# The head of a two-layer encoder kernel: three small loads on another queue, the first weights in halves, first products and scaling on ScalarE, wide matmuls ahead of the narrow sums

## The chip, the cores and the metric

The kernel runs on one NeuronCore of a Trainium2 chip. The metric is the device time of one execution in microseconds (us), as the median of several runs. TensorE (PE) multiplies matrices, VectorE (DVE), ScalarE (ACT) and GpSimd (POOL) work on elements, and SyncE (SP) issues transfers from device memory. Each engine takes its instructions in the order of the program; semaphores order the engines among each other.

## The reference

Input x is 256 tokens by 1024 features, fp32; c is one conditioning vector of 1024. Two layers, each a SwiGLU FFN with half weight, a token mixer and a second FFN. Every sub-layer is wrapped as follows; `mod` comes from c.

```python
mod = (silu(c) @ ada_w[i] + ada_b[i]).reshape(B, 9, D)      # per layer: 9 vectors of 1024
def modulated_sublayer(x, mod, g_pre, g_post, fn, weight):  # shift, scale, gate = mod[0:3] of the sub-layer
    h = rmsnorm(x, g_pre) * (1.0 + scale) + shift
    y = rmsnorm(fn(h), g_post)
    return x + weight * (1.0 + gate) * y
def swiglu(h, w_in, w_out):
    gate, up = split(h @ w_in, 2)
    return (silu(gate) * up) @ w_out                        # w_in 1024 x 5632, w_out 2816 x 1024
```

The change touches only the head of the program: the first sub-layer's shift (vector 0) and scale (vector 1), the first h, and the first products of FFN 0.

## The kernel before

The 256 tokens are two blocks of 128 (t = 0, 1). The FFN's hidden units go in 11 chunks of 256 (c = 0 to 10); a chunk's `wi` weights come in two parts of 1 MB (q = 0: k of 0 to 3, q = 1: k of 4 to 7). Most matmuls are done in three fp32r products: a weight is cast to a high part on ScalarE (L263) and the rest is its low part, subtracted on VectorE (L271); h is split in the same way (L588, L590 and L593). The three products are L98 to L100. The first parts of chunks 0 and 2 (`task_in_whole`) are used unsplit as fp32 (L794).

A modulation vector is a product of silu(c) with a 1024 x 1024 block of `ada_w`. It is not done on TensorE. The rows of the block lie as (partition, k), and VectorE adds eight products of a weight tile with one column of `sc` (`ada_step`: k = 0 writes the accumulator at L350, k = 1 to 7 add to it at L352). Narrow matmuls of one column (`finish_cols`, L361) then sum over the partitions, and two small VectorE instructions (L374, L377) add bias and norm weight. In the head the vectors are made in halves of 512 columns (`ada_half`; hf = 0, 1), each in two loads of 1 MB (q = 0, 1): vectors 0 and 1, first halves, then their second halves.

h itself: ScalarE squares x and sums (L508), VectorE and GpSimd make the root (L501, L503), x is scaled to xr in halves on ScalarE (L554) and VectorE (L555), TensorE transposes it (`turn_half`, L562), and shift and scale are applied while it is read from PSUM, on ScalarE (L576) or VectorE (L582) (`mod_half`). The rest is cast and subtracted as above.

The order is written out by hand. `Bulk` holds a list of tasks (key, load, high, low). Loads are issued by SP in the order of the list, as soon as one of 4 buffers (`N_RAW`) is free; `until(key)` runs tasks up to one, and for each emits its high part (ScalarE) and its low part (VectorE). `finish_pe` emits the narrow sums of finished vectors, `finish` also the additions behind them. `head_first` emits the first four k of chunks 0, 1 and 2 for both blocks (12 of 24 products each in chunk 1; L794 for the others), and at each `next(halves)` goes on in the generator `first_halves`, which places the other work of the head between those products. `warm` emits products of the identity with itself that nobody reads (L108).

Of the kernel before, what the change touches and what calls it, by code (L numbers as in the profile page):

```python
# [11 lines left out]
F32 = mybir.dt.float32  # L12
# [5 lines left out]
P = 128  # L18
D = 1024
S = 256  # L20
NT = S // P
KD = D // P
# [17 lines left out]
def kernel(  # L40
# [71 lines left out]


    c_col = cpool.tile([P, KD], F32, name="c_col")
    nc.sync.dma_start(c_col, c_in.rearrange("o (p k) -> p (o k)", k=KD))
    xt = [rowp.tile([P, D], F32, tag=f"x{t}", name=f"x{t}", bufs=1) for t in range(NT)]

    def load_x(t):
        nc.sync.dma_start(xt[t], x_in[0, t * P : (t + 1) * P, :])
# [8 lines left out]
    mhalf = cpool.tile([P, 1], F32, name="mhalf")  # L128
    nc.vector.memset(mhalf, -0.5)
    sc = cpool.tile([P, KD], F32, name="sc")  # L130
    nc.scalar.activation(sc, c_col, AF.Silu)


    cols = cpool.tile([P, 96 + 144 + 3], F32, name="cols")
# [1 line left out]
    C_Q = 96 + 144  # L136
    C_KV = C_Q + 2

    def load_columns(parts, base):
        rows = rowp.tile([P, 512], F32, tag="bc", name="rows", bufs=4)[:, :P]  # L140
        n = 0
        for ap in parts:
            r = ap.shape[0]
            nc.sync.dma_start(rows[n : n + r, :], ap)
            n += r

        def turn():
            ps = tr_tile("ps_cols")
            nc.tensor.transpose(ps[:, :n], rows[:n, :], ident[:n, :n])
            nc.vector.tensor_copy(cols[:, base : base + n], ps[:, :n])  # L150

        return turn

    turn_g = load_columns([norm_g.rearrange("l m (j p) -> (l m j) p", p=P)], 0)
    turn_b = load_columns([ada_b[0:1, :].rearrange("l (r p) -> (l r) p", p=P)], C_B)

    def load_columns_late():
        return load_columns(
# [157 lines left out]
    def ada_half(layer, m, hf, accs, pieces=(1, 1)):  # L316
# [16 lines left out]
        def compute(q):  # L333
            def go():
                rv = st.pop(q).rearrange("p (k n) -> p k n", k=4)
                if m not in accs:
                    accs[m] = rowp.tile([P, D], F32, tag="acc", name=f"aacc{layer}{m}", bufs=3)
                acc = accs[m][:, hf * 512 : (hf + 1) * 512]
                for j in range(4):
                    ada_step(acc, rv[:, j, :], 4 * q + j)  # L340
                if q == 1:
                    bulk.fin.append(lambda: finish_cols(layer, m, range(hf * 4, hf * 4 + 4))(acc))

            return go

        return [(("adah", m, hf, q), load(q), None, compute(q)) for q in range(2)]

    def ada_step(acc, w, k):
        if k == 0:
# [265 lines left out]
    class FFN:  # L615
# [168 lines left out]
        def head_first(self, hT, h0, halves):  # L784
# [3 lines left out]
            for c in range(3):  # L788
                if c > 0:
                    a = acc_tile(c - 1, f"first{c}")  # L790
                for t in range(NT):
                    pss[c, t] = psum.tile([P, 512], F32, tag="in", name=f"in0{t}") if c == 0 else a[t]
                    for k in range(4) if c != 1 else ():
                        nc.tensor.matmul(  # L794
                            pss[c, t], lhsT=h0[t][:, k * P : (k + 1) * P], rhs=self.wi[c, 0][:, k, :],
                            start=k == 0, stop=False,
                        )
                    if c == 1:
                        self.mm_in(pss[c, t], c, t, hT[t], range(4))
                    next(halves)  # L800
# [528 lines left out]


    accs = {}
    first = ada_half(0, 0, 0, accs) + ada_half(0, 1, 0, accs, (1, 2))
    with_load = lambda t, f: (t[0], lambda: (t[1](), f()), *t[2:])
    first[1] = with_load(first[1], lambda: load_x(0))
    first[2] = with_load(first[2], lambda: load_x(1))
    h01, h11 = ada_half(0, 0, 1, accs), ada_half(0, 1, 1, accs, (1, 2))
    first += [f0.task_in_whole(0, 0), h01[0], f0.task_in(1, 0), h01[1], *h11, f0.task_in_whole(2, 0)]
    ss1 = shift_scale(0, 1)
    first += [f0.task_in(0, 1), ss1[0], f0.task_in(1, 1), ss1[1], f0.task_in(2, 1), f0.task_out(0)]
    first += [ss1[2], f0.task_out(1), ss1[3], f0.task_in(3, 0), f0.task_in(3, 1)]  # L1340
# [50 lines left out]
        )  # L1391


    bulk.until(("adah", 0, 0, 1))
    turn_g()
    turn_b()
    bulk.finish_pe()
    s20 = first_rstd(0)
    xr0 = pre_xr(0, s20)
    bulk.until(("adah", 1, 0, 0))  # L1400
    bulk.finish()
    s21 = first_rstd(1)
    xr1 = pre_xr(1, s21)
    hT = [new_hT(0), new_hT(1)]
    turned = [turn_half(0, 0, xr0)]
    warm(6, "acc11", 1)
    turned += [turn_half(1, 0, xr1, psum.tile([P, 512], F32, tag="acc10", name="ps_h10", bufs=1))]
    warm(4, "acc11", 1)
    bulk.until(("adah", 1, 0, 1))
    bulk.finish()  # L1410
    parts = [mod_half(t, 0, ps, hT[t], 0, 0, t == 1) for t, ps in enumerate(turned)]

    def first_halves():
        bulk.until(("adah", 0, 1, 0))
        yield
        for high, low, _ in parts:
            high()
            low()
        bulk.until(("wi", 0, 0, 1, 0))
        yield  # L1420
        bulk.until(("adah", 0, 1, 1))
        bulk.finish()
        late = [turn_half(0, 1, xr0)]
        yield
        yield
        bulk.until(("adah", 1, 1, 1))
        f0.high_in(0, 1)
        bulk.finish()
        late += [turn_half(1, 1, xr1)]
        late = [mod_half(t, 1, ps, hT[t], 0, 0, t == 0) for t, ps in enumerate(late)]  # L1430
# [2 lines left out]
        for _, low, _ in late:  # L1433
            low()
        yield
        yield

    f0.head_first(hT, [p[2] for p in parts], first_halves())
    turn_late = load_columns_late()
    f0.unit(3, 0, hT[0])  # L1440
    f0.unit(3, 1, hT[1])
# [238 lines left out]
```

## Time and profile before

| | us |
|---|---|
| median of 3 runs | 925.85 (924.13 to 928.99) |
| profiled execution | 930.35 |
| its span on the core | 928.6 |
| first wide matmul of FFN 0 starts | 24.04 |
| second halves' last narrow sums start | 44.09 |
| low part of wi01 starts on VectorE | 48.94 |

Times in the trace count from the start of the span. The profiled execution is one execution, 4.5 us above the median of the runs.

### The profile page before, as it was taken

What the parts mean: (1) busy time and instruction counts of PE and PEld (TensorE: products, weight loads), DVE (VectorE), ACT (ScalarE), POOL (GpSimd) and SP (SyncE); (2) the same over time, 40 slices, a digit from 0 to 9 for tenths busy, and PEclk for the clock granted to TensorE, in tenths of its full rate; (3) what the DMA queues carried; (4) which work ended last, traced back from release to release, by engine and by line L of the source; (5) the groups of instructions that cost most, each with busy time, mean ns of one, the idle gap of its engine ahead of it and who ended that gap; (6) DMA issues with size and microseconds to landing.
All of it is one profiled execution on the core that took longest, in us unless ns stands there. A gap on an engine that the chain in (4) does not pass through costs nothing.

```text
span 928.6 us, 11171 instructions
## 1 busy us (share of the span) xinstructions
PE 898.9 (97%) x4251; PEld 733.0 (79%) x4251; DVE 703.9 (76%) x848; ACT 437.3 (47%) x653; POOL 41.8 (5%) x56
## 2 busy tenths in 40 slices
PE   3999999999999999999999999999999999999997
PEld 3568887887888888888888888888776888888885
DVE  5798888887877898797867987766798765656553
ACT  2255443345645434334742534337698654343421
POOL 0000000000000000000000000001163000000000
PEclk9899999999999999999999999998999999999999
DMA  9989998996357999898469999961143458857601
GB/s 325 368 299 343 360 373 313 351 359 242 137 180 264 378 339 326 297 387 275 137 183 360 324 351 327 344 229 59 46 137 113 160 153 280 293 193 259 227 1 45
DMA packets 135973, 235.28 MB, mean 253 GB/s; under 512 B 5628, under 2 KB 98415, under 8 KB 135664
## 3 DMA queue, kind: packets, MB, share of 16 engines
q1 hardware_dynamic: 135920, 234.58, 72.8%
q8 instruction: 33, 0.54, 0.2%
q14 instruction: 20, 0.16, 0.1%
HBM read 233.51 MB, written 1.05 MB: 253 GB/s over the span
## 4 chain that ended last, share of the span: by engine, by line
PE 88%; DVE 7%; issue 2%; DMA 1%; ACT 1%; POOL 0%; SPq 0%; DVEq 0%; POOLq 0%; ACTq 0%
PE acc L747 25%; PE in L100 16%; PE in L98 16%; PE in L99 16%; PE accm L1319 2%; PE ps_g L724 2%; DVE aacc L352 1%; PE ps_h L562 1%; PE ps_mod L361 1%; PE in L794 1%; DVE nm L1220 1%; DVE ql L1203 1%; DMA wo<-in_ffn_w_out_dram 1%; PE accp L965 1%; DMA adah<-in_ada_w_dram 1%
## 5 line engine op out<-in xcount | busy, mean ns | idle before, releaser
L352 DVE SCALAR_TENSOR_TENSOR aacc<-ada,sc,aacc 128x1024 f32<-128x1024 f32 (+1 forms) x113 | 143.8, 1272 | 9.9 <-DMA ada<-in_ada_w_dram 7.6
L708 ACT ACTIVATE sil<-in 128x256 f32<-128x256 f32 x84 | 32.2, 383 | 247.0 <-PE in L100 242.1
L710 DVE TENSOR_TENSOR g<-in,sil 128x256 f32<-128x256 f32 x84 | 35.2, 419 | 52.0 <-ACT sil L708 51.9
L95 DVE TENSOR_TENSOR gL<-ps_g,gH 128x256 fp32r<-128x256 f32 x88 | 36.6, 416 | 23.6 <-ACT gH L94 23.5
L94 ACT CAST gH<-ps_g 128x256 fp32r<-128x256 f32 x88 | 32.4, 368 | 44.5 <-PE ps_g L724 44.4
L503 POOL TENSOR_TENSOR r<-ms,mhalf 128x1 f32<-128x1 f32 x24 | 13.6, 565 | 840.5 <-DVE ms L501 840.5
L724 PEld LDWEIGHTS ps_g<-ident,g 128*128 128x128 f32 x176 | 24.7, 140 | 11.5
L724 PE MATMUL ps_g<-ident,g 128*128 128x128 f32 x176 | 33.6, 272 | 0.0
L508 ACT ACTIVATE junk<-x 128x512 bf16<-128x512 f32 x24 | 15.1, 631 | 21.1 <-DVE x L535 11.3
L361 PE MATMUL ps_mod<-ones,aacc 128*128 128x1 f32 x96 | 12.9, 262 | 10.9 <-DVE cols L150 9.7
L361 PEld LDWEIGHTS ps_mod<-ones,aacc 128*128 128x128 f32 x96 | 13.2, 213 | 11.9 <-DVE cols L150 10.0
L576 ACT ACTIVATE hs<-ps_h,mod,mod 128x128 f32<-128x128 f32 x48 | 18.0, 456 | 8.6 <-DVE mod L377 5.5
L352 DVE SCALAR_TENSOR_TENSOR aacc<-adah,sc,aacc 128x512 f32<-128x512 f32 x28 | 21.0, 751 | 0.9
L582 DVE TENSOR_SCALAR hs<-ps_h,mod,mod 128x128 f32<-128x128 f32 x48 | 16.4, 403 | 4.9 <-PE ps_h L562 4.6
L535 DVE SCALAR_TENSOR_TENSOR x<-tmp,r,x 128x512 f32<-128x512 f32 x23 | 16.3, 748 | 2.2 <-POOL r L503 1.2
L1238 POOL TENSOR_SCALAR p<-p,rs 128x256 f32<-128x256 f32 x16 | 16.1, 1008 | 26.8 <-ACT p L1228 16.4
L1228 ACT ACTIVATE p<-s,nm 128x256 f32<-128x256 f32 x32 | 15.0, 478 | 4.0 <-DVE nm L1220 2.6
L554 ACT ACTIVATE xr<-x,r 128x512 f32<-128x512 f32 x12 | 8.7, 722 | 17.4 <-POOL r L503 17.4
L593 DVE TENSOR_TENSOR hTL<-hs,hTH 128x512 fp32r<-128x512 f32 x24 | 15.6, 689 | 0.4
L271 DVE TENSOR_TENSOR wo10L<-wo,wo10H 128x2048 fp32r<-128x2048 f32 x4 | 9.2, 2292 | 8.1 <-ACT wo10H L263 8.1
L397 DVE TENSOR_REDUCE mod<-ps_turn 128x4 f32<-128x512 f32 x12 | 8.2, 687 | 8.1 <-PE ps_turn L391 8.1
L562 PE MATMUL ps_h<-ident,xr 128*128 128x128 f32 x96 | 13.7, 283 | 0.5 <-ACT xr L554 0.3
(498 smaller groups left out, 2880.3 us busy)
## 6 DMA issues: line engine op xcount, KB each, us to landing
wi<-in_ffn_w_in_dram SPq DMA_DIRECT2D x176, 512.0 KB, 5.8
ada<-in_ada_w_dram SPq DMA_DIRECT2D x64, 1024.0 KB, 7.1
wo<-in_ffn_w_out_dram SPq DMA_DIRECT2D x44, 1024.0 KB, 6.4
adah<-in_ada_w_dram SPq DMA_DIRECT2D x6, 1024.0 KB, 10.3
mwo<-in_mla_w_o_dram SPq DMA_DIRECT2D x4, 1024.0 KB, 6.1
bc<-in_ada_b_dram SPq DMA_DIRECT2D x12, 256.0 KB, 6.8
bc<-in_norm_g_dram SPq DMA_DIRECT2D x12, 256.0 KB, 7.4
adah<-in_ada_w_dram SPq DMA_DIRECT2D x4, 512.0 KB, 11.7
```

The lines of the kernel that those rows point to most:

```text
L94: nc.scalar.copy(h, src)
L95: nc.vector.tensor_sub(lo, src, h.bitcast(F32))
L98: nc.tensor.matmul(ps, lhsT=lh, rhs=rh, start=first, stop=False)
L99: nc.tensor.matmul(ps, lhsT=lh, rhs=rl, start=False, stop=False)
L100: nc.tensor.matmul(ps, lhsT=ll, rhs=rh, start=False, stop=last)
L352: nc.vector.scalar_tensor_tensor(acc, w, sc[:, k : k + 1], acc, op0=ALU.mult, op1=ALU.add)
L361: nc.tensor.matmul(ps[:, j : j + 1], lhsT=acc[:, (j - j0) * P : (j - j0 + 1) * P], rhs=ones[:, 0:1], start=True, stop=True,)
L562: nc.tensor.transpose(ps[:, j * P : (j + 1) * P], xr[:, kk * P : (kk + 1) * P], ident)
L708: nc.scalar.activation(sil, ps[:, 0:CW], AF.Silu)
L710: nc.vector.tensor_mul(g, ps[:, CW : 2 * CW], sil)
L724: nc.tensor.transpose(ps[:, a * P : (a + 1) * P], g[:, a * P : (a + 1) * P], ident)
L747: nc.tensor.matmul(acc[hf], lhsT=lhs[:, a, :], rhs=rhs[:, a, hf * 512 : (hf + 1) * 512], start=f, stop=l)
```

## The change

The loads of c, of the norm weights and of the first layer's biases go from SP's queue to ScalarE's; the Silu is emitted after them. The transposes of norm weights and biases (`turn_g`, `turn_b`) come before the first modulation products. The first four modulation loads are each made in two pieces of 512 KB (the fourth already was), and x of block 1 is loaded after all of them. The product with k = 0 of the half vectors is made on ScalarE, as the task's high part. Both halves of xr are scaled on ScalarE. The ten identity products are replaced by five of 512 columns with x, all behind the transposes of block 0; the second block's root, scaling, transposes and shift come later, its transposes inside chunk 0 of `head_first`. In the list, `wi` chunk 1 comes ahead of vector 0's second half. In `first_halves` the narrow sums of the second halves and what hangs on them come one or two steps later: those of vector 0 after the first block of chunk 2, those of vector 1 after its second block.

```diff
--- before.py
+++ after.py
@@ -112,7 +112,7 @@
 
 
     c_col = cpool.tile([P, KD], F32, name="c_col")
-    nc.sync.dma_start(c_col, c_in.rearrange("o (p k) -> p (o k)", k=KD))
+    nc.scalar.dma_start(c_col, c_in.rearrange("o (p k) -> p (o k)", k=KD))
     xt = [rowp.tile([P, D], F32, tag=f"x{t}", name=f"x{t}", bufs=1) for t in range(NT)]
 
     def load_x(t):
@@ -128,7 +128,6 @@
     mhalf = cpool.tile([P, 1], F32, name="mhalf")
     nc.vector.memset(mhalf, -0.5)
     sc = cpool.tile([P, KD], F32, name="sc")
-    nc.scalar.activation(sc, c_col, AF.Silu)
 
 
     cols = cpool.tile([P, 96 + 144 + 3], F32, name="cols")
@@ -136,12 +135,12 @@
     C_Q = 96 + 144
     C_KV = C_Q + 2
 
-    def load_columns(parts, base):
+    def load_columns(parts, base, queue=nc.sync):
         rows = rowp.tile([P, 512], F32, tag="bc", name="rows", bufs=4)[:, :P]
         n = 0
         for ap in parts:
             r = ap.shape[0]
-            nc.sync.dma_start(rows[n : n + r, :], ap)
+            queue.dma_start(rows[n : n + r, :], ap)
             n += r
 
         def turn():
@@ -151,8 +150,10 @@
 
         return turn
 
-    turn_g = load_columns([norm_g.rearrange("l m (j p) -> (l m j) p", p=P)], 0)
-    turn_b = load_columns([ada_b[0:1, :].rearrange("l (r p) -> (l r) p", p=P)], C_B)
+    turn_g = load_columns([norm_g.rearrange("l m (j p) -> (l m j) p", p=P)], 0, nc.scalar)
+    turn_b = load_columns([ada_b[0:1, :].rearrange("l (r p) -> (l r) p", p=P)], C_B, nc.scalar)
+
+    nc.scalar.activation(sc, c_col, AF.Silu)
 
     def load_columns_late():
         return load_columns(
@@ -333,17 +334,20 @@
         def compute(q):
             def go():
                 rv = st.pop(q).rearrange("p (k n) -> p k n", k=4)
-                if m not in accs:
-                    accs[m] = rowp.tile([P, D], F32, tag="acc", name=f"aacc{layer}{m}", bufs=3)
                 acc = accs[m][:, hf * 512 : (hf + 1) * 512]
-                for j in range(4):
+                for j in range(q == 0, 4):
                     ada_step(acc, rv[:, j, :], 4 * q + j)
                 if q == 1:
                     bulk.fin.append(lambda: finish_cols(layer, m, range(hf * 4, hf * 4 + 4))(acc))
 
             return go
 
-        return [(("adah", m, hf, q), load(q), None, compute(q)) for q in range(2)]
+        def first():
+            if m not in accs:
+                accs[m] = rowp.tile([P, D], F32, tag="acc", name=f"aacc{layer}{m}", bufs=3)
+            nc.scalar.activation(accs[m][:, hf * 512 : (hf + 1) * 512], st[0][:, 0:512], AF.Copy, scale=sc[:, 0:1])
+
+        return [(("adah", m, hf, q), load(q), first if q == 0 else None, compute(q)) for q in range(2)]
 
     def ada_step(acc, w, k):
         if k == 0:
@@ -791,6 +795,8 @@
                 for t in range(NT):
                     pss[c, t] = psum.tile([P, 512], F32, tag="in", name=f"in0{t}") if c == 0 else a[t]
                     for k in range(4) if c != 1 else ():
+                        if c == 0 and t == 0 and k == 2:
+                            next(halves)
                         nc.tensor.matmul(
                             pss[c, t], lhsT=h0[t][:, k * P : (k + 1) * P], rhs=self.wi[c, 0][:, k, :],
                             start=k == 0, stop=False,
@@ -1329,12 +1335,12 @@
 
 
     accs = {}
-    first = ada_half(0, 0, 0, accs) + ada_half(0, 1, 0, accs, (1, 2))
+    first = ada_half(0, 0, 0, accs, (2, 2)) + ada_half(0, 1, 0, accs, (2, 2))
     with_load = lambda t, f: (t[0], lambda: (t[1](), f()), *t[2:])
     first[1] = with_load(first[1], lambda: load_x(0))
-    first[2] = with_load(first[2], lambda: load_x(1))
+    first[3] = with_load(first[3], lambda: load_x(1))
     h01, h11 = ada_half(0, 0, 1, accs), ada_half(0, 1, 1, accs, (1, 2))
-    first += [f0.task_in_whole(0, 0), h01[0], f0.task_in(1, 0), h01[1], *h11, f0.task_in_whole(2, 0)]
+    first += [f0.task_in_whole(0, 0), f0.task_in(1, 0), *h01, h11[0], f0.task_in_whole(2, 0), h11[1]]
     ss1 = shift_scale(0, 1)
     first += [f0.task_in(0, 1), ss1[0], f0.task_in(1, 1), ss1[1], f0.task_in(2, 1), f0.task_out(0)]
     first += [ss1[2], f0.task_out(1), ss1[3], f0.task_in(3, 0), f0.task_in(3, 1)]
@@ -1391,40 +1397,53 @@
         )
 
 
-    bulk.until(("adah", 0, 0, 1))
     turn_g()
     turn_b()
+    bulk.until(("adah", 0, 0, 1))
     bulk.finish_pe()
     s20 = first_rstd(0)
-    xr0 = pre_xr(0, s20)
+    r0 = rstd(s20, 1.0)
     bulk.until(("adah", 1, 0, 0))
     bulk.finish()
-    s21 = first_rstd(1)
-    xr1 = pre_xr(1, s21)
+    xr0 = rowp.tile([P, D], F32, tag="xr", name="xr0")
+    for hf in range(2):
+        nc.scalar.activation(xr0[:, hf * 512 : (hf + 1) * 512], xt[0][:, hf * 512 : (hf + 1) * 512], AF.Copy, scale=r0)
     hT = [new_hT(0), new_hT(1)]
     turned = [turn_half(0, 0, xr0)]
-    warm(6, "acc11", 1)
-    turned += [turn_half(1, 0, xr1, psum.tile([P, 512], F32, tag="acc10", name="ps_h10", bufs=1))]
-    warm(4, "acc11", 1)
+    scratch = psum.tile([P, 512], F32, tag="acc11", name="warm", bufs=1)
+    for _ in range(5):
+        nc.tensor.matmul(scratch, lhsT=ident, rhs=xt[0][:, 0:512], start=True, stop=True)
     bulk.until(("adah", 1, 0, 1))
+    r1 = rstd(first_rstd(1), 1.0)
     bulk.finish()
-    parts = [mod_half(t, 0, ps, hT[t], 0, 0, t == 1) for t, ps in enumerate(turned)]
+    xr1 = rowp.tile([P, D], F32, tag="xr", name="xr1")
+    for hf in range(2):
+        nc.scalar.activation(xr1[:, hf * 512 : (hf + 1) * 512], xt[1][:, hf * 512 : (hf + 1) * 512], AF.Copy, scale=r1)
+    parts = [mod_half(0, 0, turned[0], hT[0], 0, 0, False)]
+    h_first = [parts[0][2]]
 
     def first_halves():
-        bulk.until(("adah", 0, 1, 0))
+        ps = turn_half(1, 0, xr1, psum.tile([P, 512], F32, tag="acc10", name="ps_h10", bufs=1))
+        parts.append(mod_half(1, 0, ps, hT[1], 0, 0, True))
+        h_first.append(parts[1][2])
+        yield
         yield
         for high, low, _ in parts:
             high()
             low()
+        f0.high_in(1, 0)
         bulk.until(("wi", 0, 0, 1, 0))
+        bulk.until(("adah", 0, 1, 0))
         yield
         bulk.until(("adah", 0, 1, 1))
-        bulk.finish()
+        yield
+        bulk.until(("adah", 1, 1, 0))
+        yield
+        bulk.finish_pe()
         late = [turn_half(0, 1, xr0)]
-        yield
-        yield
         bulk.until(("adah", 1, 1, 1))
         f0.high_in(0, 1)
+        yield
         bulk.finish()
         late += [turn_half(1, 1, xr1)]
         late = [mod_half(t, 1, ps, hT[t], 0, 0, t == 0) for t, ps in enumerate(late)]
@@ -1433,9 +1452,8 @@
         for _, low, _ in late:
             low()
         yield
-        yield
-
-    f0.head_first(hT, [p[2] for p in parts], first_halves())
+
+    f0.head_first(hT, h_first, first_halves())
     turn_late = load_columns_late()
     f0.unit(3, 0, hT[0])
     f0.unit(3, 1, hT[1])
```

## Rows read from the trace of the kernel before

**Rows 1.** The page, part 4: engines' shares of the chain that ended last.

```profile
PE 88%; DVE 7%; issue 2%; DMA 1%; ACT 1%; POOL 0%; SPq 0%; DVEq 0%; POOLq 0%; ACTq 0%
```

**Rows 2.** TensorE's longest wait, 20 to 110 us: total, times, longest.

```profile
PE acc L747 <- DVE g L710: 1.1, 1, 1.1
```

**Rows 3.** Timeline of SP: start, us, engine, line, operation, count.

```profile
0.72 0.38 SPq L115 DMA_DIRECT2D c_col<-in_c_dram  x1
...
2.11 0.94 SPq L328 DMA_DIRECT2D adah<-in_ada_w_dram  x2
...
51.30 0.92 SPq L626 DMA_DIRECT2D wi<-in_ffn_w_in_dram  x2
```

**Rows 4.** Timeline of VectorE, 0 to 52 us; brackets: idle before, releaser.

```profile
7.44 0.48 DVE L350 TENSOR_SCALAR aacc<-adah,sc 128x512 f32<-128x512 f32 x1 [6.07 <-DMA adah<-in_ada_w_dram]
7.96 5.47 DVE L352 SCALAR_TENSOR_TENSOR aacc<-adah,sc,aacc 128x512 f32<-128x512 f32 x7
...
13.66 0.15 DVE L501 SCALAR_TENSOR_TENSOR ms<-s 128x1 f32<-128x1 f32 x1
...
29.29 2.28 DVE L271 TENSOR_TENSOR wi10L<-wi,wi10H 128x2048 fp32r<-128x2048 f32 x1
...
47.27 0.41 DVE L588 CAST hTH<-hs 128x512 fp32r<-128x512 f32 x1
...
48.94 2.28 DVE L271 TENSOR_TENSOR wi01L<-wi,wi01H 128x2048 fp32r<-128x2048 f32 x1
```

**Rows 5.** Timeline of ScalarE, 0 to 30 us.

```profile
0.72 1.28 ACT L131 ACT_TABLE_LOAD   x1 [0.72 <-PEq L1667]
...
11.35 0.63 ACT L508 ACTIVATE junk<-x 128x512 bf16<-128x512 f32 x1 [8.64 <-DMA x<-in_x_dram]
...
12.64 0.19 ACT L508 ACTIVATION_READ_ACCUMULATOR junk<-x 128x1 f32 x1
14.47 0.72 ACT L554 ACTIVATE xr<-x,r 128x512 f32<-128x512 f32 x1 [1.64 <-POOL r L503]
...
23.64 1.50 ACT L576 ACTIVATE hs<-ps_h,mod,mod 128x128 f32<-128x128 f32 x4 [4.39 <-DVE mod L377]
25.02 0.63 ACT L590 CAST hTH<-hs 128x512 fp32r<-128x512 f32 x1
26.85 1.90 ACT L263 CAST wi10H<-wi 128x2048 fp32r<-128x2048 f32 x1 [1.21 <-DMA wi<-in_ffn_w_in_dram]
```

**Rows 6.** Timeline of TensorE, 15 to 45 us; two records per fp32 matmul.

```profile
15.38 1.09 PE L562 MATMUL ps_h<-ident,xr 128*128 128x128 f32 x4
16.27 2.77 PE L108 MATMUL warm<-ident 128*128 128x128 f32 x12
...
19.91 1.06 PE L108 MATMUL warm<-ident 128*128 128x128 f32 x8
22.09 1.06 PE L361 MATMUL ps_mod<-ones,aacc 128*128 128x1 f32 x8 [1.12 <-DVE aacc L352]
24.04 6.12 PE L794 MATMUL in<-wi,hs 128*128 128x512 f32 x7 [0.90 <-DVE hs L582]
...
40.66 3.59 PE L794 MATMUL first<-wi,hs 128*128 128x512 f32 x8
44.09 0.95 PE L361 MATMUL ps_mod<-ones,aacc 128*128 128x1 f32 x8
```

**Rows 7.** Stretches (from:to, us): busy engines, then granted clock, DMA share, GB/s.

```profile
8.00:10.00 2.00, 0.00 (x0) 0.00 (x0) 1.93 (x3) 0.00 (x0) 0.00 (x0) 1.00 1.06 406
...
23.00:23.50 0.50, 0.15 (x2) 0.50 1.09 367
...
29.50:30.00 0.50, 0.50 (x2) 0.68 1.06 393
```

**Rows 8.** The chain of waits, 0 to 100 us: one product of chunk 1.

```profile
34.03 0.23 PE first L98
```

**Rows 9.** DMA issues, 0 to 75 us: count, KB each, us to landing.

```profile
c_col<-in_c_dram SPq DMA_DIRECT2D x1, 4.0 KB, 1.8
```

## The prediction

> **What bounds the kernel now.** I began with the page: TensorE holds 88% of the chain that ended last [rows 1], so time is won only where TensorE idles or runs at its slower clock. Then the waits of TensorE: after the first wide matmul only one long wait is left up to 110 us, the 1.1 us for the first down-projection [rows 2]. Everything the change can touch therefore lies before about 66 us. Next the queues there, engine by engine. SP issues three small loads first, so the first modulation weights are issued at 2.11 us instead of 0.72 [rows 3]. VectorE waits for them until 7.44 and then makes one 512-column product every 0.78 us (seven in 5.47) [rows 4]. TensorE's first wide matmul starts at 24.04, 1.95 us after the narrow sums of the second vector (22.09) [rows 6]. Last the clock. The column of granted clock reads 1.00 before 23 us, but the identity products tell it apart: 12 records in 2.77 us from 16.27, 0.23 each, and 8 in 1.06 us from 19.91, 0.13 each [rows 6]. So TensorE is at the 1.2 GHz level until about 19, at 2.4 after it, at 1.2 again from 23.0 (granted 0.50), and back to 2.4 between 29.5 and 30 (0.68 in that half microsecond) [rows 7]. Before it fell it had idled 1.1 us, run narrow sums and idled 0.9 us [rows 6]. From 24.04 to about 29.7, 5.66 us of wide work run at half rate: 2.83 us lost.
>
> A landmark is needed that both programs share. I take the second pair of narrow sums (L361 at 44.09) [rows 6]. After them both have the same code: last half of h, its casts, the low part of wi01 (ends 48.94 + 2.28 = 51.22, that is 7.13 us later) [rows 4], and at 51.30 SP issues the next weights, whose buffer that instruction frees [rows 3]. The first down-projection weights come from that stream and TensorE then waits for them [rows 2]. So a shift of the landmark shifts the end by as much, in either direction.
>
> **Up to the first wide matmul.** Three small loads go to ScalarE's queue: the weights start 1.39 us earlier (0.72 for 2.11) [rows 3]. The first 1 MB took 5.3 us from its issue to its use (2.11 to 7.44) [rows 3, 4], and at 406 GB/s [rows 7] a MB takes 2.6 to 2.7; so the n-th MB of the queue lands near 0.72 + 2.6 + 2.7n: the first half load at 4.7, x0 (after 2.5) at 10.1, the second vector's first half (3.0) at 11.4 and last (4.5) at 15.5, wi00 (6.0) at 19.5, wi10 (7.0) at 22.2. On ScalarE three issues (0.4 each, as on SP [rows 3]) and a table load of 1.28 [rows 5] end near 3.3 and the Silu near 3.6, so the k=0 product waits for the weights, not the reverse. That product costs 0.72 on ScalarE, by the nearest row, the 512-column scaling of x [rows 5], and removes a 0.48 us step from VectorE [rows 4]. VectorE starts k=1 at about 5.6 rather than 7.96; seven steps of 0.78 end at 11.1. The squares of x0 end at 10.1 + 1.48 = 11.6 (11.35 to 12.83 before [rows 5]), the root another 0.81 later (13.66 to 14.47 [rows 4, 5]), at 12.4. ScalarE is by then just done with the k=0 product of the second vector (11.7 to 12.45), and xr0's first half ends at 13.25. The second vector: its product at 12.45, seven steps of 0.78 and 0.2 for a small addition between them, done near 18.1 (22.09 before).
>
> But TensorE now stands elsewhere. It transposes the first half from 13.3 (1.09 at the slow level [rows 6]) and from 14.4 runs five 512-column fp32 products that nobody reads, ahead of the narrow sums in its queue. The trace has no such product with that operand; the nearest is L794, fp32 and 512 columns, two records each: 6.12 us for the first seven records at half clock, 0.87 each, and 3.59 for eight at full clock, 0.43 each as they follow one another [rows 6]. Ten records cost 4.3 us if all are fast and 8.7 if all are slow; they end between 18.7 and 23.1. The two rises seen came about 4 us (15.38 to 19.3) and 5.66 us after dense work began, so I put this one at 17.3 to 19.0 and the end at 20.2 to 21.1; I take 20.6. That is 2.5 us behind VectorE's 18.1, so everything won there (products on ScalarE, both halves of xr on ScalarE, one rstd moved back, the split loads) lies under the five products. If that cover were gone, wide work would start at 18.1 + 1.95 = 20.05. With it: 20.6 + 1.95 = 22.55, 1.5 us earlier than 24.04. The weights wi00 are there by 19.5 and don't decide.
>
> The Trainium skill ("TensorE: Matmul & The Clock Gate", Part 4: PE-mode transpose) says that transposes don't count as activity for the clock. The rows can't separate this, because transposes and identity products follow each other there; by that rule the rise would come about 1 us later and the sum would be 0.5 us higher.
>
> **From there to the landmark.** I take the clock to stay at 2.4 GHz: between dense work and wide work lie 1.95 us, against 3.07 (20.97 to 24.04) when it fell. Both ends are kept: 0 and, if it falls again, 2.83 us. First chunk: 16 records of 0.43, 6.9 us, and inside it now the four transposes of the second block (half of 1.09, 0.55): done at +7.4 after the first wide matmul. The second chunk needs the low part of wi10. Its chain: two products (1.72), transposes (0.55), ScalarE's four scalings (1.50), its cast of h (0.63), its cast of wi10 (1.90) [rows 5], VectorE's subtraction (2.28) [rows 4], with gaps +8.65. So TensorE gets a new wait of about 1.0 us. This chain, not the landing, sets it: wi10 has moved ahead of a modulation load and lies ready from 22.2. Then 23 of 24 products of 0.23 [rows 8], 5.25; third chunk's first block 3.44; narrow sums 0.95 and transposes 0.55; and, new ahead of the last narrow sums, the third chunk's second block, 3.44. Sum: 8.65 + 5.25 + 3.44 + 0.95 + 0.55 + 3.44 = 22.3. The landmark falls at 22.55 + 22.3 = 44.85 against 44.09: 0.75 us late. VectorE isn't the limit: its 14 products between wi10's low part (31.2) and the landmark end near 42.1. Behind that low part SP holds h11's second half (same buffer) and with it all later loads: issued at 31.2 it is there by 36.5, 5.3 later, and wanted at 39. The wide block put ahead of the sums is the cost. Before, it ran behind the sums and covered the work on h; now nothing covers it.
>
> **After the landmark.** From the narrow sums to the first cast of the last half (44.09 to 47.68, 3.6 us [rows 4, 6]) TensorE has only those sums and four transposes, longer than the 3.07 us in which the clock fell before. I assume that it falls, another 2.83 us at most. Cover: TensorE arrives 1.3 us ahead of wi01's low part and waits 1.1 us for the down-projection [rows 2], so 0.4 reaches the end (0 if it doesn't fall, 2.8 without the cover). Total: 0.75 + 0.4 = about 1.15 us later.
>
> **The sum.** The profiled execution took 930.35 us (span 928.6 and 1.75 around it), so it would become 931.5. The runs shown have median 925.85, 4.5 below that execution; carried over: 927.0.
>
> **Rivals.** First, the clock falls ahead of the first chunk. For: a light stretch of 1.95 us is left, in which the sums are one column wide. Against: five dense products just before it, and a shorter stretch than 3.07. Price: 2.83 if it rises within 5.66 us as it did; if the transposes inside the chunk spoil that, all 16 records at 0.87 instead of 0.43, 7.0, of which the 1.0 wait for wi10 is covered: 6.0. That gives 929.8 to 933.0, and from a price of 3.5 on it is slower by over 0.5% (4.6 us, about what a measurement of this kernel can tell from no change).
>
> Second, it is faster. TensorE reaches 2.4 GHz before the five products (they end at 18.7, wide start 20.65, 1.9 earlier), and the last stretch keeps its clock (0.4): 1.15 - 1.9 - 0.4 gives 924.7; without the new wait of 1.0 as well, 923.7. For: the column reads 1.00 there. Against: the 0.23 us records under the same 1.00.
>
> Third, the split does not do what it is there for. A 4 KB load alone takes 1.8 us from issue to landing [rows 9]; if each of the three extra pieces (three loads of the first four are cut anew) paid that and nothing overlapped, VectorE would end 5.4 us later (23.5), wide work would start at 25.45 instead of 22.55 and the time be 927.0 + 2.9 = 929.9. Against: by the issues, pieces queue behind one another. If instead the first product waits for both pieces, 1.3 us are lost at VectorE, and the 2.5 us cover hides them.
>
> The Trainium skill ("DMA: Bandwidth & Descriptors", Bandwidth) advises loads of 1 MiB or more, which speaks against the halves. By its fit of 2.0 us plus bytes over 436 GB/s three more pieces would cost 6 us if none overlapped, an estimate close to this rival's 5.4.
>
> **Chances.** Forecast 0.65, clock falls early 0.20 (half of it beyond 4.6 us), faster 0.12, pieces 0.03. The forecast's own range is 924.5 to 929. The range that takes in the others runs from 922.8 (the faster rival, less half of the 1.7 by which the lowest run shown lies under the median) to 931.4 (middle of the first rival). Faster by over 0.5% needs 3 us more than any term here gives: 0.07. Slower: half of the first rival and a little of the others, 0.12. Within: 0.81.
>
> **What would show it.** First weights issued near 0.7; first wide matmul at 22 to 23, behind the dense products and not behind VectorE; granted clock 1.00 in the first chunk; a 1 us wait of the second chunk on wi10L; the second narrow sums near 45; wi01L ending near 52. I am wrong if the wide start is at 20 or earlier, if the clock reads 0.50 in the first chunk, or if the landmark and the end do not move together.

## The result and the profile after

| | before | changed |
|---|---|---|
| median, us | 927.7 (6 runs, 924.13 to 928.99) | 932.45 (6 runs, 931.82 to 934.69) |
| ratio of the changed kernel, 95% interval | | 1.0051 [1.0031, 1.0072] |
| profiled execution, us (span) | 930.35 (928.6) | 934.69 (932.9) |

The changed kernel is slower by 4.75 us between the medians. The forecast was 927.0, with a range to 931.4, so the time lies outside the range by 1 us. Two further lots of both kernels (below; a lot is a set of executions of several kernels on one chip) give 1.0019 and 1.0032; what the three intervals share is 1.0031 to 1.0037, about 3 us. The ratio is not the quotient of the two medians: in the two further lots the medians differ by only 1.8 and 1.4 us. So the change costs time in every lot, and its size is known only roughly.

TensorE's timeline of the changed kernel, 5 to 55 us, answers to [rows 6]. Lines have moved: L365 are the narrow sums (L361 before), L566 the transposes (L562), L800 the unsplit products (L794), L1415 the new dense products.

```profile
5.87 0.40 PE L148 MATMUL ps_cols<-ident,rows 96*128 96x96 f32 x1 [5.87 <-DMA rows<-in_norm_g_dram]
6.44 0.38 PE L148 MATMUL ps_cols<-ident,rows 72*128 72x72 f32 x1 [0.17 <-DMA rows<-in_ada_b_dram]
12.53 1.86 PE L365 MATMUL ps_mod<-ones,aacc 128*128 128x1 f32 x8 [5.71 <-DVE aacc L356]
14.42 1.12 PE L566 MATMUL ps_h<-ident,xr 128*128 128x128 f32 x4
15.33 6.63 PE L1415 MATMUL warm<-x,ident 128*128 128x512 f32 x10
21.80 0.95 PE L365 MATMUL ps_mod<-ones,aacc 128*128 128x1 f32 x8
23.64 1.98 PE L800 MATMUL in<-wi,hs 128*128 128x512 f32 x4 [0.89 <-DVE hs L586]
25.46 0.60 PE L566 MATMUL ps_h<-ident,xr 128*128 128x128 f32 x4
25.90 5.32 PE L800 MATMUL in<-wi,hs 128*128 128x512 f32 x12
...
32.28 0.50 PE L99 MATMUL first<-wi10L,hTH 128*128 128x512 f32 x1 [0.84 <-DVE wi10L L272]
...
37.64 3.59 PE L800 MATMUL first<-wi,hs 128*128 128x512 f32 x8
41.07 0.95 PE L365 MATMUL ps_mod<-ones,aacc 128*128 128x1 f32 x8
...
42.35 3.60 PE L800 MATMUL first<-wi,hs 128*128 128x512 f32 x8
45.79 0.95 PE L365 MATMUL ps_mod<-ones,aacc 128*128 128x1 f32 x8
...
49.44 1.26 PE L814 MATMUL in<-wi01H,hTH 128*128 128x512 f32 x4 [1.79 <-DVE hTH L592]
...
52.97 2.08 PE L814 MATMUL in<-wi01L,hTH 128*128 128x512 f32 x4 [0.56 <-DVE wi01L L272]
```

The wide work starts at 23.64, behind the dense products (ended near 21.9), and 16 records of it take 7.6 us with the transposes inside: full clock. The second chunk waits for wi10L. The second block of chunk 2 (42.35) now stands ahead of the last narrow sums, the landmark, which start at 45.79. Behind them TensorE stands idle twice, 0.25 and 1.79 us, and the four products from 52.97 take 2.08 us, half speed.

VectorE of the changed kernel, against [rows 4]:

```profile
6.30 0.26 DVE L149 COPY cols<-ps_cols 128x96 f32<-128x96 f32 x1 [4.93 <-PE ps_cols L148]
6.86 0.23 DVE L149 COPY cols<-ps_cols 128x72 f32<-128x72 f32 x1 [0.30 <-PE ps_cols L148]
7.01 5.46 DVE L356 SCALAR_TENSOR_TENSOR aacc<-adah,sc,aacc 128x512 f32<-128x512 f32 x7
...
29.94 2.29 DVE L272 TENSOR_TENSOR wi10L<-wi,wi10H 128x2048 fp32r<-128x2048 f32 x1
32.15 10.86 DVE L356 SCALAR_TENSOR_TENSOR aacc<-adah,sc,aacc 128x512 f32<-128x512 f32 x14
...
50.63 2.28 DVE L272 TENSOR_TENSOR wi01L<-wi,wi01H 128x2048 fp32r<-128x2048 f32 x1
...
158.67 2.28 DVE L272 TENSOR_TENSOR wi81L<-wi,wi81H 128x2048 fp32r<-128x2048 f32 x1
```

ScalarE of the changed kernel, against [rows 5]:

```profile
1.20 0.50 ACTq L143 DMA_DIRECT2D rows<-in_norm_g_dram  x1
1.72 0.67 ACTq L143 DMA_DIRECT2D rows<-in_ada_b_dram  x1
...
4.70 0.72 ACT L348 ACTIVATE aacc<-adah,sc 128x512 f32<-128x512 f32 x1 [0.18 <-DMA adah<-in_ada_w_dram]
```

The k = 0 product runs at 4.70, but k = 1 starts on VectorE only at 7.01: two copies out of PSUM, which hang on the small loads, stand ahead of it.

Stretches of the changed kernel (columns as in [rows 7], here with the busy times of all five engines; the third number from the end is the granted clock):

```profile
8.00:10.00 2.00, 0.00 (x0) 0.00 (x0) 1.93 (x3) 0.00 (x0) 0.00 (x0) 1.00 1.03 400
23.00:24.00 1.00, 0.36 (x1) 0.30 (x2) 0.96 (x4) 0.00 (x0) 0.00 (x0) 1.00 1.04 385
...
51.00:52.00 1.00, 1.00 (x4) 0.60 (x2) 1.00 (x1) 0.51 (x1) 0.00 (x0) 0.50 0.00 0
...
234.00:238.00 4.00, 4.00 (x12) 2.91 (x12) 2.77 (x4) 2.32 (x2) 0.00 (x0) 0.59 0.01 2
```

The clock that fell at 23 before [rows 7] stays up, and falls at 50 to 58 instead. The chain of waits of the changed kernel shows what reaches the first down-projection:

```profile
1.72 4.67 DMA rows<-in_ada_b_dram
...
68.16 2.78 PE acc L751 x11
```

The same step of before starts at 65.78, so the head alone brings 2.4 us in this pair of executions.

### The profile page after: what moved, and what is told of

It is laid out like the page before. It is cut to its first block, busy times and chain, and to the rows that moved or that the text cites. A ratio compares the mean times of both kernels' runs of the same rounds, so it can differ in the third digit from the quotient of the medians.

```text
span 932.9 us, 11163 instructions
## 1 busy us (share of the span) xinstructions
PE 904.0 (97%) x4241; PEld 734.3 (79%) x4241; DVE 701.3 (75%) x842; ACT 440.8 (47%) x659; POOL 42.2 (5%) x56
## 4 chain that ended last, share of the span: by engine, by line
PE 89%; DVE 6%; issue 2%; ACT 1%; DMA 1%; POOL 0%; ACTq 0%; DVEq 0%; POOLq 0%
PE acc L751 25%; PE in L100 16%; PE in L98 16%; PE in L99 16%; PE accm L1325 2%; PE ps_g L728 2%; PE ps_h L566 1%; PE ps_mod L365 1%; PE accp L971 1%; DVE nm L1226 1%; DVE ql L1209 1%; PE first L800 1%; PE warm L1415 1%; PE in L814 1%; DVE aacc L356 1%
## 5 line engine op out<-in xcount | busy, mean ns | idle before, releaser
L365 PEld LDWEIGHTS ps_mod<-ones,aacc 128*128 128x128 f32 x96 | 12.5, 203 | 7.4 <-DVE aacc L356 5.9
L365 PE MATMUL ps_mod<-ones,aacc 128*128 128x1 f32 x96 | 12.1, 253 | 5.7 <-DVE aacc L356 5.7
L566 PE MATMUL ps_h<-ident,xr 128*128 128x128 f32 x96 | 14.7, 297 | 0.3 <-DVE mod L378 0.3
L566 PEld LDWEIGHTS ps_h<-ident,xr 128*128 128x128 f32 x96 | 12.5, 156 | 2.1 <-issue 0.7
```

The lines of the kernel that those rows point to most:

```text
L365: nc.tensor.matmul(ps[:, j : j + 1], lhsT=acc[:, (j - j0) * P : (j - j0 + 1) * P], rhs=ones[:, 0:1], start=True, stop=True,)
L566: nc.tensor.transpose(ps[:, j * P : (j + 1) * P], xr[:, kk * P : (kk + 1) * P], ident)
```

## The experiments

Each ratio is against the kernel before on the same chip. One point far behind the head is read from all traces: the start of wi81's low part on VectorE, ahead of the later light stages. It is called the far mark.

**Repeats: is the loss the kernel's or the execution's?** Both kernels unaltered, in two further lots, and one more trace of the kernel before.

> The changed kernel, unaltered, for a second trace. Placement theory (the wide block ahead of the sums, the new wait and the late light stretch cost 2.4 us at the end of the head, and two half-clock stretches in the pool mixer, 1.7 and 1.6 us, come on top because everything runs 2.4 us later): 4 to 5 us slower than before, the same two pool stretches at half clock near 235 and 255 us, first wide matmul at 23.6, second narrow sums at 45.8. Rival (the two pool stretches were chance in one execution): 2.4 to 3 us slower in the median, and the second trace has them elsewhere or not.

> The kernel before, unaltered, for a second trace and for what a comparison of a kernel with itself shows. Both theories: ratio 1.000 within 0.2%. If the half-clock stretches in the light stages are fixed by the program, the trace repeats them (full clock at 230 to 237 us, half near 238 to 240, half for 1.6 us near 655); if they are chance, they move between the two traces by a microsecond or more.

> The changed kernel, unaltered, for the size of the change with a third lot of executions. If the size is what the traces show against the two kinds of head of the kernel before (2.4 us behind the one that lost its clock in the first chunk, 4.4 behind the one that kept it): 2.5 to 3.5 us slower in the median, the ratio between the two earlier ones (1.0019 and 1.0051). If the first measurement was right by itself: 4.5 us or more; if the second: under 2.

> The kernel before, unaltered, for a third trace. If the fall of the clock ahead of the first chunk (seen in the first trace, last narrow sums at 44.1, and not in the second, 42.0) is a matter of the execution: either of the two again, and nothing between but for the place of the rise. If it belongs to one chip: kept, as in the second.

Measured: the changed kernel 930.72 against 928.94, ratio 1.0019 [1.0001, 1.0037], and 929.87 against 928.48, ratio 1.0032 [1.0012, 1.0052]. The kernel before against itself: 928.38, ratio 1.000 [0.9987, 1.0013]; its third trace is of an execution of 926.71. TensorE in the second trace of before:

```profile
23.79 7.13 PE L794 MATMUL in<-wi,hs 128*128 128x512 f32 x16 [0.90 <-DVE hs L582]
...
42.03 0.95 PE L361 MATMUL ps_mod<-ones,aacc 128*128 128x1 f32 x8
```

Here all 16 records of the first chunk take 7.13 us; in the trace that I predicted from, the first seven alone took 6.12 [rows 6]. The third trace of before lies between:

```profile
23.78 8.83 PE L794 MATMUL in<-wi,hs 128*128 128x512 f32 x16 [0.90 <-DVE hs L582]
...
42.66 0.95 PE L361 MATMUL ps_mod<-ones,aacc 128*128 128x1 f32 x8
```

In the first trace the 16 records took 9.99 us. So the clock cost the first chunk 2.86, 0 and 1.70 us in three executions of one program: the loss of the first trace is not a fixed cost of that kernel. The landmark of before lies at 44.09, 42.03 and 42.66, mean 42.93. The changed kernel's lies at 45.79, 45.85 and 44.37, mean 45.34: 2.4 us later. Its third trace differs in the dense products:

```profile
15.13 5.41 PE L1415 MATMUL warm<-x,ident 128*128 128x512 f32 x10
...
22.22 1.98 PE L800 MATMUL in<-wi,hs 128*128 128x512 f32 x4 [0.89 <-DVE hs L586]
```

The dense products took 5.41 us instead of 6.63, and wide work starts 1.4 us earlier: the time at which the clock rises within them varies too. The far mark lies at 156.29, 153.66 and 154.03 before (mean 154.66) and at 158.67, 158.73 and 155.88 changed (157.76): 3.1 us later. In the kernel before:

```profile
156.29 2.28 DVE L271 TENSOR_TENSOR wi81L<-wi,wi81H 128x2048 fp32r<-128x2048 f32 x1
```

Two of the three traced executions of the changed kernel are among its longest (934.69 and 934.85; the third took 928.55), so this mean may stand high. The run times give a similar size. Over all lots those of the kernel before with a mean granted clock of 0.992 have a median of 928.50 (38 of them), those of the changed kernel at the same clock 931.62 (8): 3.1 us. At 0.990 and 0.993 it is 2.9 and 2.6.

On the stretches in the pool mixer neither theory holds as written. The second trace of the changed kernel repeats the one at 234 to 238 us (granted 0.61), the third doesn't (1.00). When the work arrives doesn't decide it alone: with the landmark at 44.37 (third trace) the stretch was granted 1.00, with the landmark at 44.38 (the run with the small loads' transposes moved, below) 0.80.

**A delay in the head of the kernel before.** Three products that nobody reads, on VectorE behind the first eight:

```diff
     bulk.until(("adah", 0, 0, 1))
+    for _ in range(3):
+        nc.vector.scalar_tensor_tensor(accs[0][:, 512:1024], xt[0][:, 0:512], sc[:, 0:1],
+                                       xt[0][:, 512:1024], op0=ALU.mult, op1=ALU.add)
```

> The kernel before with three idle VectorE products of 0.78 us put behind the first eight modulation products: all that follows starts 2.3 us later, with nothing else changed (no part of the computation is left out). If a shift of the head reaches the end one to one: 2.3 us slower. If the clock in later light stretches depends on when they fall: anything from 0 to 6 us slower, with other half-clock stretches in the pool mixer than in the trace of before. If the head's shift is absorbed later: 0 to 1 us slower.

Measured: 932.26 against 928.94, ratio 1.0036 [1.0019, 1.0052]. The wide start moves from 23.79 to 26.02 with the clock kept (7.13 for the 16 records), the landmark from 42.03 to 44.25, the far mark from 153.66 to 156.54. So 2.2 us at the wide start are 2.2 at the landmark, 2.9 at the far mark and 3.3 in the median (1.8 to 4.8 by the interval): a shift of the head does reach the end, and the interval leaves no room for one that is mostly absorbed.

**The order at the landmark.** In the changed kernel the last narrow sums and what hangs on them are emitted ahead of chunk 2's second block again:

```diff
         f0.high_in(0, 1)
-        yield
         bulk.finish()
...
             low()
         yield
+        yield
```

> The changed kernel with the last narrow sums and the last half of h back ahead of chunk 2's second wide block, as in the kernel before. Placement theory: the sums start at 43.0 (when VectorE's products end) instead of 45.8, the wide block covers the work on h, the clock stays at 2.4 GHz until wi01's products, wi01's low part ends at 50.1 instead of 52.9, the end of the head comes 3 us earlier than in the changed kernel: 1.5 to 2 us faster than it, or more if the pool clock returns (0 to 1 us from the kernel before). Rival (the cost is the late start of the first chunk, behind the dense products and the small loads): no more than 0.5 us faster than the changed kernel.

Measured: 928.06 against 928.94, ratio 0.9995 [0.9979, 1.0011]; the changed kernel in the same lot 930.72. TensorE:

```profile
42.90 1.05 PE L365 MATMUL ps_mod<-ones,aacc 128*128 128x1 f32 x8 [0.61 <-DVE mod L378]
...
44.70 3.60 PE L800 MATMUL first<-wi,hs 128*128 128x512 f32 x8
47.73 1.49 PE L814 MATMUL in<-wi01H,hTH 128*128 128x512 f32 x4
```

The sums come at 42.90, the block of 3.60 covers the work on h behind them, and the wait of 1.79 for hTH is gone. The half-clock stretch at 50 is gone in this trace too, but two runs below keep the wait and have no half clock there, so the wait alone doesn't bring it. From wide start to landmark are 19.50 us instead of 22.15. The landmark, 42.90, and the far mark, 154.78, are then those of the kernel before (42.93 and 154.66 in the mean): in the trace this one move gives back 2.7 us at the landmark and leaves nothing of the loss. The medians agree (2.7 us below the changed kernel in the same lot, more than the 1.8 that the change costs there), but the two intervals overlap.

No changed kernel ran in the lot of the next three runs and of the fourth move below; they are held against its ratios in the other lots, 1.0019 to 1.0051, and its three traces.

**The transposes of the small loads.** `turn_g` and `turn_b` behind the first products, as before the change:

```diff
-    turn_g()
-    turn_b()
     bulk.until(("adah", 0, 0, 1))
+    turn_g()
+    turn_b()
```

> The changed kernel with one part undone: the transposes of norm weights and biases stand behind the first eight modulation products again. If their late rows (landed at 5.87 and 6.44 us in the changed kernel) hold up the head: VectorE starts the products near 5.5 instead of 7.0, the first narrow sums run near 11, the block transposes start near 13.3 instead of 14.4, first wide matmul at 22.6 instead of 23.6, and the time is 1 us below the changed kernel's. If the dense products and the clock set the start whatever comes first: wide start within 0.3 us of 23.6 and no change.

Measured: 930.1 against 928.36, ratio 1.0013 [1.0, 1.0027]. TensorE:

```profile
11.14 1.86 PE L365 MATMUL ps_mod<-ones,aacc 128*128 128x1 f32 x8 [4.41 <-DVE cols L149]
13.36 1.11 PE L566 MATMUL ps_h<-ident,xr 128*128 128x128 f32 x4 [0.35 <-ACT xr L1410]
14.27 6.29 PE L1415 MATMUL warm<-x,ident 128*128 128x512 f32 x10
```

k = 1 starts at 5.33 instead of 7.01 and the transposes of x at 13.36, the forecast's 13.3. The dense products start 0.65 to 1.06 us earlier than in five traces that keep these transposes ahead (14.92 to 15.33). The wide start, 22.24, lies within the changed kernel's own 22.22 to 23.69. The ratio lies below the changed kernel's, by no more than the lots differ among themselves, so what this is worth at the end isn't shown.

**The dense products.** Left out (their result is read by nobody):

```diff
-    scratch = psum.tile([P, 512], F32, tag="acc11", name="warm", bufs=1)
-    for _ in range(5):
-        nc.tensor.matmul(scratch, lhsT=ident, rhs=xt[0][:, 0:512], start=True, stop=True)
```

> The changed kernel without the five dense products that nobody reads (the output is unaffected). If they cover VectorE and pay for themselves in clock: wide start near 21 instead of 23.6, but the first chunk at half clock for some 5.7 us, so that the second chunk starts at about the same time (within 0.5 us of 32.3) and the end moves by less than 1 us. If they are the cost of the change: the second chunk starts 2.5 us earlier and the time falls by 2 to 3 us.

Measured: 930.92 against 928.36, ratio 1.0021 [1.0003, 1.0039]. TensorE:

```profile
18.47 1.84 PE L365 MATMUL ps_mod<-ones,aacc 128*128 128x1 f32 x8 [2.54 <-DVE aacc L356]
21.20 3.78 PE L800 MATMUL in<-wi,hs 128*128 128x512 f32 x4 [0.90 <-DVE hs L586]
...
45.56 0.95 PE L365 MATMUL ps_mod<-ones,aacc 128*128 128x1 f32 x8
```

Without them VectorE releases the sums at 18.47, but the first four records take 3.78 us instead of 1.98. The second chunk's first L99 product comes at 32.06 (32.28 with the dense products) and the landmark at 45.56: the earlier start (2.44 us) and the slower clock (1.80 on four records, 0.46 on the transposes) cancel, since the transposes, the casts and the subtraction for wi10 behind those four records set the second chunk either way. The ratio is among the changed kernel's.

**The wait on wi10.** Its task emitted at the start of `first_halves`:

```diff
     def first_halves():
+        f0.high_in(1, 0)
+        bulk.until(("wi", 0, 0, 1, 0))
...
             low()
-        f0.high_in(1, 0)
-        bulk.until(("wi", 0, 0, 1, 0))
```

> The changed kernel with wi10's cast on ScalarE and its low part on VectorE ahead of the second block's scalings, in idle time of both engines. If the new wait of chunk 1 for that low part costs what the trace shows: no wait at the second chunk (0.84 us and what stands before it, 1.4 in all, gone), last narrow sums at 44.4 instead of 45.8, 1 to 1.5 us faster than the changed kernel. If the wait only hides a later one: landmark earlier by under 0.5 us, time unchanged.

Measured: 929.98 against 928.36, ratio 1.0026 [1.0013, 1.0039]. The low part runs at 25.46, L99 comes without a wait, and from wide start (23.22) to landmark (44.26) are 21.04 us instead of 22.15 (the landmark was forecast at 44.4). TensorE:

```profile
44.26 0.95 PE L365 MATMUL ps_mod<-ones,aacc 128*128 128x1 f32 x8
...
48.95 1.07 PE L814 MATMUL in<-wi01H,hTL 128*128 128x512 f32 x4
51.44 1.19 PE L814 MATMUL in<-wi01L,hTH 128*128 128x512 f32 x4 [1.43 <-DVE wi01L L272]
```

At wi01L TensorE now waits 1.43 instead of 0.56. That doesn't take the gain back: wi01L starts 4.84 us behind the landmark in both, and TensorE only arrives earlier, as its products ahead of the wait keep full clock here (1.07 for 1.91 us); without the dense products, at full clock too, it waits 1.42. The median doesn't show the 1.1 us: the ratio lies among the changed kernel's.

**Together.** The three moves (sums first, transposes of the small loads later, wi10 early) in one kernel; the same without the dense products; and the three with wi01's low part ahead of the additions as well (`bulk.until(("wi", 0, 0, 0, 1))` behind `f0.high_in(0, 1)`).

> The changed kernel with three orders mended (last sums ahead of the second block of chunk 2, norm weights' transposes behind the first products, wi10 split early), and without the early low part of wi01, whose late landing held up VectorE and with it the sums in the kernel with all four. If that wait was what spoilt it: no wait above 1 us before the down-projection, last sums near 40 to 41, wi01's low part ending near 48, no clock fall before 230 us, 2 to 3 us faster than the kernel before. If the mended orders gain nothing at the end: within 1 us of the kernel before.

> The same without the five dense products. If they only move the half-clock stretch: wide start near 20, first chunk at half clock, last sums within 0.5 us of the other, same time within 1 us. If they cost once nothing else holds the head: 2 us faster.

> The changed kernel with four orders mended together: last narrow sums ahead of the second block of chunk 2, transposes of norm weights behind the first products, wi10 split early, and wi01's low part in VectorE's idle time ahead of the last sums. If the order of the head is the whole cost: wide start 22.6, last sums near 41, no half-clock stretch before 230 us, first down-projection near 60 to 61 (67.5 in the changed kernel, 62 to 64 before), 5 to 7 us faster than the changed kernel and 3 to 5 faster than the kernel before. If something else in the change costs (transfers, the clock in later light stretches): no better than 1 us below the kernel before.

Measured: 926.84 (ratio 0.9984 [0.9967, 1.0002]) and 926.83 (0.9989 [0.9974, 1.0004]) against 928.48, with the changed kernel at 929.87 in the same lot; the version with the fourth move 931.93 against 928.36, 1.0043 [1.0021, 1.0065]. TensorE with three moves:

```profile
22.00 1.98 PE L800 MATMUL in<-wi,hs 128*128 128x512 f32 x4 [0.90 <-DVE hs L586]
...
39.84 1.05 PE L365 MATMUL ps_mod<-ones,aacc 128*128 128x1 f32 x8
...
41.99 4.94 PE L800 MATMUL first<-wi,hs 128*128 128x512 f32 x8
46.37 1.49 PE L814 MATMUL in<-wi01H,hTH 128*128 128x512 f32 x4
```

The landmark is 3.1 us earlier than the mean of before, wi01's high products 0.4 to 1.0 earlier than in the second and third trace of before (46.76, 47.39), as the block behind the sums now runs partly at half clock (4.94 for 3.60). The median is 1.6 us lower, with an interval that just touches 1. The forecast of 2 to 3 us wasn't reached, nor the one of no clock fall before 230 us. Without the dense products the time is the same, though the landmark lies at 41.28 and not within 0.5 us: there the block behind the sums keeps full clock (3.60).

The fourth move was my mistake: slower than the kernel before by 3.6 us, where 3 to 5 faster was expected. VectorE with it:

```profile
43.21 2.29 DVE L272 TENSOR_TENSOR wi01L<-wi,wi01H 128x2048 fp32r<-128x2048 f32 x1 [3.06 <-ACT wi01H L264]
45.42 0.15 DVE L378 TENSOR_TENSOR mod<-ps_mod,cols 128x4 f32<-128x4 f32 x1
```

VectorE waits 3.06 us for ScalarE's cast, the small addition stands behind it, and TensorE's last sums wait 4.74 us for that addition. The moved instruction's wait was inherited by all that is queued behind it.

## Why the prediction was off

**What held.** Weights were issued at 0.72 and used at 4.70. The pieces show no cost: seven products took 5.46 us against 5.47 [rows 4], VectorE was done with the second vector at 17.93 (forecast 18.1), and the queue moved 400 GB/s against 406 [rows 7]; no run undoes the pieces alone. The Trainium skill's rule of 1 MiB ("DMA: Bandwidth & Descriptors", Bandwidth) was the one that spoke against them; here the trace doesn't bear it out. The Trainium skill's fit that the prediction used beside it stands on the same page under Anatomy of one DMA — SWDGE (gpsimd) path, and is measured for that path; these loads were issued by SyncE. The dense products, not VectorE, set the wide start; the clock read 1.00 in the first chunk; the second chunk waited for wi10L (0.84 us, about 1.0 forecast); VectorE's 14 products ended at 43.0, ahead of the landmark; 7.12 us lay between the landmark and wi01L's end, as before; the clock fell in the late light stretch. The block put ahead of the sums was named as the cost, and in the run that moved it back the loss at the landmark and the far mark is gone. So the mechanism was right, and its size was not.

**The step that failed** is in "The sum": "The profiled execution took 930.35 us ... so it would become 931.5 ... carried over: 927.0". The forecast credited the change with 2.83 us for keeping the clock in the first chunk. That loss belonged in this size to the profiled execution, not to the kernel: three traces lost 2.86, 0 and 1.70 us there, 1.5 in the mean. The change was set against an execution with its landmark at 44.09, and the difference then carried over to a median of three runs that lay 4.5 us below that execution and 1.85 below the median of six. Against the mean landmark of three traces, 42.93, the same steps would have given 44.85 - 42.93 = 1.9 instead of 0.75 at the landmark. The text itself held the sign of it, 4.5 us between the execution and the median, and made nothing of it.

**Two smaller terms.** The landmark of the changed kernel is at 45.34 in the mean, not 44.85. The excess lies ahead of the wide start (23.18 in the mean, 22.55 forecast). One cause is the late start of the dense products, and that comes from the small loads, as the run that moved their transposes shows (0.65 to 1.06 us); how much of it reaches the landmark isn't shown. Issued on ScalarE at 1.20, the norm weights were used at 5.87; on SP's queue ahead of the weights they landed 2.1 us after issue. I moved the loads and the transposes that use them, and did not count what then stood ahead of k = 1 on VectorE (7.01 instead of 5.6). Behind its products came the root (12.39) and the first vector's narrow sums (12.53 to 14.39), and the transposes of x stand behind both (14.42 instead of 13.3). The Trainium skill says that DMAs from several engines run on the same 16 DMA engines and interleave, and that issuing from several engines saves only the time of issuing ("DMA: Bandwidth & Descriptors", Issuing engines are not separate DMA queues); the trace agrees: 1.39 us of issue saved for the weights, and 4.67 us to landing for the 36 KB of biases beside them. After the landmark the mean loss is 0.69 (3.10 at the far mark less 2.41) where 0.4 was put. It is 1.15 in the two traces in which the late half-clock stretch lasts to about 58 us; in the third, which is back at full clock by 51.5, the far mark lies as far behind the landmark as in the kernel before (111.5 us; there 111.4 to 112.2).

**The account.** 1.15 forecast + 1.16 (44.09 less 42.93) + 0.49 (landmark) + 0.29 (behind it) = 3.1 us. That this is the far mark's shift is so by construction; it lies at the upper end of the shift at equal clock and within what the three intervals share.

**The time itself** missed by 5.45 us. With 3.1 for the change that is 1.85 because the median of before is 927.7 with six runs (928.4 to 928.9 in the other lots) and not 925.85; 1.95 from the account above; and 1.65 that is left over in the first lot. There the six executions of the changed kernel had mean clocks of 0.988 to 0.992, where others reach 0.997 and 926.9 us. In the first pair of traces a part of it shows as half-clock stretches far behind the change: granted 0.59 at 234 to 238 us, where the first trace of before reads 1.00 and its second 0.57. Why that lot drew so many of them isn't shown.

**The rivals.** The clock didn't fall ahead of the first chunk in any trace of the changed kernel. The pieces show no cost. It wasn't faster: the second rival needed 2.4 GHz before the five dense products, and they took 5.41 to 6.86 us in the eight traces that have them, where ten fast records would take 4.3. By the Trainium skill's rule on transposes ("TensorE: Matmul & The Clock Gate", Part 4: PE-mode transpose) the wide start would be later. It was, but the late small loads and the varying rise of the clock can explain that without the rule, and no run separates it.

**What stays open:** in what share of its executions the kernel before loses clock in the first chunk (two of three traces here), what the change costs more closely than some 1.4 to 4.75 us, and what decides where a half-clock stretch falls. Whether the change with three moves beats the kernel before isn't settled at 1.6 us.

## What to carry to other kernels

A loss that is seen in one profiled execution is a credit for a change only as far as further executions of the same kernel show it too; where the profiled execution lies above the median of the runs, take that first as a warning. Before a wide block is put ahead of narrow work, ask what covered the wait behind that narrow work until now: here the block itself did. When a load moves to another queue, put its first use behind the work that needn't wait for it, or everything queued behind that use inherits the load's delay.

## What the runs showed of the hardware

I hadn't expected one program to differ by so much on one chip: in one lot the kernel before took 924.57 to 931.48 us and the changed kernel 926.88 (mean granted clock 0.997) to 934.85 (0.988). That is 0.7 and 0.9%, more than the change itself, and the time goes with the mean clock. The same span of time falls to half clock in one execution and not in the next: 234 to 238 us was granted 1.00, 0.57 and 1.00 in the three traces of before. Nor had I expected that a few wide products ahead of the first chunk would buy nothing: they hold the clock at 2.4 GHz (1.98 against 3.78 us for four records), and the time is the same without them (926.84 and 926.83 us with the three moves).
